# A decoder layer on one core: negated attention scores, and the second half's left output projection ahead of the first norms

## The chip, the cores and the metric

The kernel runs on one core of a Trainium2 chip. The metric is the device time of one execution in microseconds (us); lower is better. The kernel before takes 1022.47 us, the median of 3 runs (1022.22 to 1023.44). The engines are PE (TensorE), DVE (VectorE), ACT (ScalarE), POOL (GpSimd) and SP (SyncE, which here only issues DMAs). Each works off its own queue of instructions in order.

## The reference

One layer of a hybrid decoder on 1024 tokens of width 1024, in float32:

```python
z = h @ w_in                       # pool group | q | k | v
y_pool = pool_mixer(u_pool, w_pool, pool_scale)        # windows 2, 4, 8, 16
y_attn = sliding_window_attention(q, k, v, sinks)      # 128-token band
h = layer_norm(ALPHA * h + concat([y_pool, y_attn]) @ w_out)
h = layer_norm(ALPHA * h + square(relu(h @ w_ff1)) @ w_ff2)
h = h + sigmoid(h @ w_ple_gate + b_ple_gate) * (p @ w_ple)
```

In the attention each head has a sink, a score without a key:

```python
m = maximum(max(scores, axis=-1), sink)
e = exp(scores - m)
probs = e / (sum(e, axis=-1) + exp(sink - m))
```

## The kernel before

The tokens are handled in 8 blocks of 128 (n = 0 to 7), in two halves t of four. Every matrix product is made of three matmuls (`mm3`, lines 112 to 114): an operand is split into a rounded high part, cast on ACT (`high`, line 98), and a low part, the rest, subtracted on DVE or POOL (`low`, line 103). So a line of a trace with L98 or L103 is such a split, of whatever tile.

The stages around the change, in the order in which the program is written: query, key, value and pooling products; `attention(0)` to `attention(7)` with pooling groups between; `out_left(0)`, the left 512 columns of the output projection of blocks 0 to 3; `out_right(0)` to `(3)`, the right 512 columns; the first norms `norm1(0)` to `(3)`; `out_left(1)` and `out_right(4)` to `(7)` for the second half; then `early(0)` to `(7)`, the first products of the feed-forward part, with `norm1(4)` to `(7)` among them. A scheduler, which runs a timeline of its own, decides how instructions of neighbouring stages are mixed on each engine; it isn't a plain copy of the program's order.

`attention(n)` handles two groups of four heads. For each pair of heads there is one score tile s in PSUM (a single buffer): matmuls L283 and L284, then on DVE L287 adds the bias, takes the maximum with the sink and leaves it in `st`. L293 negates the four maxima, four exponentials (L295, ACT) use them as their bias, and DVE normalises (L299, L301); the transposes L308 follow on PE. The pooling groups use POOL and DVE for their window sums (L352, L355) and PE for `mm<-tmp,wp`.

`residual(n, ...)` (L427, DVE) adds the projection to ALPHA times the tokens in `hn[n]`, a tile of the pool "n" (`nat`, 8 buffers), one half of the columns at a time. `layer_norm` takes statistics (L393, L395) and the variance v (L397), its power -0.5 on POOL (L398), some small DVE instructions (L400 to L403), the centring on ACT (L404), and scale and shift on DVE (L405, L117). `norm1(n)` then transposes `hn[n]` in two groups of four on PE (L414), into a tile pt and a tile av in PSUM, and empties each of them by a plain copy to `raw[c]`, a high part and a low part into `X["11"]` and `X["21"]` (L513 to L516). `raw[c]` is itself a tile of the pool "n". At the end of `norm1` `hn[n]` is multiplied by ALPHA (L529, ACT) and stored to DRAM as `h_dram[n]` by a DMA that POOL issues (L530; in the profile hd). `early(0)` multiplies by the whole of `X["11"]`, so by all four blocks of the first half.

`out_left(1)` needs four weight tiles w (two buffers). In before each is loaded to a staging tile of the pool "ws", which exists only once the attention's buffers (`pa_ctx`) have been given back.

Of the kernel before, what the change touches and what calls it, by code (L numbers as in the profile page):

```python
# [7 lines left out]
F32 = mybir.dt.float32  # L8
F32R = mybir.dt.float32r
AF = mybir.ActivationFunctionType  # L10
ALU = mybir.AluOpType
# [56 lines left out]
def layer(ctx, tc, xT, x, pT, w_in, w_pool, pscale, sinks, w_out, ln1, w1, w2, ln2, w_ple, w_gate, bgate, bias, rcount, out):  # L68
# [14 lines left out]
    def wt(shape, dt=F32R):  # L83
        return sb.tile(shape, dt, tag="w", bufs=2, name=nm("w"))
# [179 lines left out]
    def attention(n):  # L264
# [4 lines left out]
        for g in range(2):  # L269
            e = pa.tile([P, 4, 2 * P + 1], F32, tag="e", bufs=2, name=nm("e"))  # L270
            st = small([P, 16])
            for j in range(2):
# [12 lines left out]
                for i in range(2):  # L285
                    h = 4 * g + 2 * j + i
                    nc.vector.tensor_tensor_reduce(  # L287
                        out=e[:, 2 * j + i, k0 : 2 * P], in0=s[:, i, k0 : 2 * P], in1=nd[:, k0 : 2 * P],
                        scale=SLOPES[h], scalar=sink_sb[:, h : h + 1], op0=ALU.add, op1=ALU.max,
                        accum_out=st[:, 2 * j + i : 2 * j + i + 1],  # L290
                    )
            nc.gpsimd.tensor_copy(out=e[:, :, 2 * P], in_=sink_sb[:, 4 * g : 4 * g + 4])
            nc.vector.tensor_scalar(out=st[:, 4:8], in0=st[:, 0:4], scalar1=-1.0, scalar2=None, op0=ALU.mult)  # L293
            for i in range(4):
                nc.scalar.activation(  # L295
                    out=e[:, i, k0 : 2 * P + 1], in_=e[:, i, k0 : 2 * P + 1], func=AF.Exp,
                    bias=st[:, 4 + i : 5 + i], scale=1.0, accum_out=st[:, 8 + i : 9 + i],
                )
# [82 lines left out]
    keys(0, first[0])  # L381
    nc.sync.dma_start(out=sink_sb, in_=sinks.partition_broadcast(P))
    nc.sync.dma_start(out=psc, in_=pscale)
    nc.sync.dma_start(out=rc, in_=rcount.partition_broadcast(P))
# [32 lines left out]
    def out_load(dst, dh, kk, st, eng):  # L417
        load_split(dst[:, 0], dst[:, 1], w_out[dh, kk], None, eng, st)
# [10 lines left out]

    def left_weights(kk, staging, eng):  # L430
        w = wt([P, 2, 2, HALF])
        out_load(w, 0, kk, staging(), eng)
        return w

    def out_left(t, staging, eng, ws=()):
        blocks = range(4 * t, 4 * t + 4)
        os = [acc_ps() for _ in blocks]
        for k in range(NK):
            if k % 2 == 0:
                w = ws[k // 2] if k // 2 < len(ws) else left_weights(k // 2, staging, eng)  # L440
            for n in blocks:
                out_mm(os[n % 4], n, k, w)
        return os

    def residual_left(t, os):
        for n in range(4 * t, 4 * t + 4):
            hn[n] = nat([P, D])
            nc.sync.dma_start(out=hn[n], in_=x[n * P : (n + 1) * P, :])
        for n in range(4 * t, 4 * t + 4):
            residual(n, 0, os[n % 4])  # L450
# [55 lines left out]
    def norm1(n):  # L506
        t, c = n // 4, n % 4
        layer_norm(hn[n], gb1)
        a = transposed(hn[n], 0, tr_ps())
        b = transposed(hn[n], 1, tr_av())  # L510
        if t == 0:
            raw[c] = nat([P, 2, 4, P])
# [4 lines left out]
        else:  # L517
# [10 lines left out]
            split_to("T4", c, t2, nc.gpsimd)  # L528
        nc.scalar.mul(out=hn[n], in_=hn[n], mul=ALPHA)  # L529
        nc.gpsimd.dma_start(out=h_dram[n], in_=hn[n])  # L530

# [16 lines left out]
    def early(p):  # L548
# [13 lines left out]
        return rest  # L562

    residual_left(0, out_left(0, lambda: stage([P, 2, HALF]), nc.gpsimd))
    for j in range(2):
# [9 lines left out]
    X["11"], X["21"] = (big([P, 2, 4, HALF]) for _ in range(2))  # L575
    by_part = (lambda: part((P, 2, HALF), F32), nc.vector)
    ws = [left_weights(kk, *by_part) for kk in range(2)]
    for n in range(4):
        norm1(n)
    residual_left(1, out_left(1, *by_part, ws))  # L580
    for n in range(4, NT):
# [343 lines left out]
```

## Time and profile before

| | |
|---|---|
| median of 3 runs | 1022.47 us |
| the profiled execution's own time | 1020.45 us |
| its span | 1018.7 us (1.75 us lie around it) |
| mean granted clock of TensorE | 0.992 |
| PE busy in the span | 994.7 us |

Times inside the execution are us from the span's start. A row of a timeline gives start, duration, engine, line, operation, output and inputs, the count of merged instructions, and in brackets the engine's idle time before it and what ended it. Rows of the waits give total, count and longest. A matmul of 512 columns shows 0.39 us, but the next one starts some 0.23 us later, since they overlap.

### The profile page before, as it was taken

What the parts mean: (1) busy time and instruction counts of PE and PEld (TensorE: products, weight loads), DVE (VectorE), ACT (ScalarE), POOL (GpSimd) and SP (SyncE); (2) the same over time, 40 slices, a digit from 0 to 9 for tenths busy, and PEclk for the clock granted to TensorE, in tenths of its full rate; (3) what the DMA queues carried; (4) which work ended last, traced back from release to release, by engine and by line L of the source; (5) the groups of instructions that cost most, each with busy time, mean ns of one, the idle gap of its engine ahead of it and who ended that gap; (6) DMA issues with size and microseconds to landing.
All of it is one profiled execution on the core that took longest, in us unless ns stands there. A gap on an engine that the chain in (4) does not pass through costs nothing.

```text
span 1018.7 us, 12237 instructions
## 1 busy us (share of the span) xinstructions
PE 994.7 (98%) x4556; PEld 824.0 (81%) x4556; DVE 707.4 (69%) x1115; ACT 458.3 (45%) x737; POOL 149.9 (15%) x180
## 2 busy tenths in 40 slices
PE   8999998989999999999999999999999999999998
PEld 6878886867888888888888888878788888888887
DVE  5778877793889676665456757787447799897433
ACT  5656656554277343443443444333433353651111
POOL 0043273620034000110000001000111120000000
PEclk9999999998999999999999999999999999999999
DMA  6421411416235233663264793656898773521011
GB/s 214 174 83 43 167 42 42 135 42 216 83 137 199 104 110 134 234 179 145 65 251 159 290 329 112 178 180 194 235 212 208 191 184 124 184 88 50 32 42 42
DMA packets 39004, 148.54 MB, mean 146 GB/s; under 512 B 4768, under 2 KB 5664, under 8 KB 36128
## 3 DMA queue, kind: packets, MB, share of 16 engines
q1 hardware_dynamic: 29664, 116.29, 33.3%
q0 software_dynamic: 9280, 31.46, 12.2%
q8 instruction: 36, 0.59, 0.2%
q14 instruction: 24, 0.20, 0.1%
HBM read 124.66 MB, written 23.07 MB: 145 GB/s over the span
## 4 chain that ended last, share of the span: by engine, by line
PE 84%; DVE 8%; DMA 5%; issue 2%; ACT 1%; POOL 0%; SPq 0%; DVEq 0%; ACTq 0%; POOLq 0%
PE f L113 20%; PE f L114 20%; PE f L112 20%; PE mm L112 7%; PE mm L113 7%; PE mm L114 6%; DMA ws<-in_w 3%; DMA w<-in_w 1%; DVE w L103 1%; DVE x L103 1%; PE pt L308 1%; DVE ws L117 1%; PE f L414 1%; PE s L283 1%; PE s L284 1%
## 5 line engine op out<-in xcount | busy, mean ns | idle before, releaser
L113 PE MATMUL f<-x,w 128*128 128x512 f32 x448 | 175.4, 392 | 3.6 <-DVE x L103 3.6
L113 PE MATMUL f<-c,ws 128*128 128x512 f32 (+1 forms) x456 | 175.9, 386 | 0.3 <-DVE c L103 0.3
L112 PE MATMUL f<-c,ws 128*128 128x512 f32 (+1 forms) x456 | 175.3, 385 | 0.0
L114 PE MATMUL f<-x,w 128*128 128x512 f32 x448 | 175.1, 391 | 0.0
L114 PE MATMUL f<-c,ws 128*128 128x512 f32 (+1 forms) x456 | 173.7, 385 | 0.0
L112 PE MATMUL f<-x,w 128*128 128x512 f32 x448 | 147.7, 390 | 0.0
L98 ACT CAST w<-st 128x1024 fp32r<-128x1024 f32 (+2 forms) x67 | 66.8, 998 | 114.3 <-issue 70.6
L103 DVE TENSOR_TENSOR w<-st,w 128x1024 fp32r<-128x1024 f32 (+2 forms) x63 | 74.9, 1192 | 43.0 <-ACT w L98 42.9
L113 PEld LDWEIGHTS f<-x,w 128*128 128x128 f32 x448 | 84.5, 189 | 22.0 <-DVE x L103 4.4
L113 PEld LDWEIGHTS f<-c,ws 128*128 128x128 f32 x456 | 85.7, 188 | 17.8 <-DVE c L103 0.7
L114 PEld LDWEIGHTS f<-c,ws 128*128 128x128 f32 x456 | 85.7, 188 | 17.2
L112 PEld LDWEIGHTS f<-c,ws 128*128 128x128 f32 x456 | 85.7, 188 | 17.1
L114 PEld LDWEIGHTS f<-x,w 128*128 128x128 f32 x448 | 84.5, 189 | 17.6
L112 PEld LDWEIGHTS f<-x,w 128*128 128x128 f32 x448 | 84.3, 188 | 17.4
L98 ACT CAST ws<-w 128x512 fp32r<-128x512 f32 x64 | 39.4, 621 | 59.5 <-PE f L114 45.9
L103 DVE TENSOR_TENSOR x<-ws,x 128x1024 fp32r<-128x1024 f32 x52 | 63.4, 1218 | 0.0
L112 PE MATMUL mm<-c,w 128*128 128x512 f32 x152 | 60.6, 403 | 1.0 <-ACT w L98 1.0
L113 PE MATMUL mm<-c,w 128*128 128x512 f32 x152 | 60.6, 400 | 0.4 <-DVE c L103 0.4
L114 PE MATMUL mm<-c,w 128*128 128x512 f32 x152 | 59.8, 398 | 0.0
L103 DVE TENSOR_TENSOR ws<-w,ws 128x512 fp32r<-128x512 f32 x64 | 46.0, 722 | 19.5 <-ACT ws L98 19.0
L98 ACT CAST ws<-st 128x512 fp32r<-128x512 f32 x48 | 29.8, 620 | 59.5 <-PE f L114 50.1
L117 DVE TENSOR_TENSOR n<-t,f 128x512 f32<-128x512 f32 x48 | 32.2, 683 | 32.0 <-PE f L114 32.0
(190 smaller groups left out, 1849.2 us busy)
## 6 DMA issues: line engine op xcount, KB each, us to landing
ws<-in_w SPq DMA_DIRECT2D x68, 512.0 KB, 3.5
w<-in_w SPq DMA_DIRECT2D x16, 1024.0 KB, 5.6
c<-fd SPq DMA_DIRECT2D x6, 2048.0 KB, 8.2
fd<-n POOLq DMA_DIRECT2D x20, 512.0 KB, 3.5
ws<-in_w POOLq DMA_DIRECT2D x20, 512.0 KB, 7.2
st<-in_w_in SPq DMA_DIRECT2D x18, 512.0 KB, 3.4
w<-in_w SPq DMA_DIRECT2D x12, 512.0 KB, 3.8
n<-in_x SPq DMA_DIRECT2D x8, 512.0 KB, 4.5
```

The lines of the kernel that those rows point to most:

```text
L98: nc.scalar.copy(out=dst, in_=src)
L103: eng.tensor_tensor(out=dst, in0=src, in1=hi.bitcast(F32), op=ALU.subtract)
L112: nc.tensor.matmul(o, ah, bh, start=first, stop=False, skip_group_check=more)
L113: nc.tensor.matmul(o, ah, bl, start=False, stop=False, skip_group_check=more)
L114: nc.tensor.matmul(o, al, bh, start=False, stop=last, skip_group_check=more)
L117: nc.vector.tensor_tensor(out=o, in0=a, in1=b, op=op)
L283: nc.tensor.matmul(s[:, i, dst], ql, kt[:, 0, g, kk : kk + kn], start=True, stop=False)
L284: nc.tensor.matmul(s[:, i, dst], ql, kt[:, 1, g, kk : kk + kn], start=False, stop=True)
L308: nc.tensor.transpose(pt[:, i, :], e[:, i, kb * P : (kb + 1) * P], ident)
L414: nc.tensor.transpose(pt[:, k, :], y[:, kt * P : (kt + 1) * P], ident)
```

## The change

Two things change. First, the scores are negated: the sinks are multiplied by -1 once after their load, L287 scales by -SLOPES and takes the minimum, and the exponential gets scale -1. The minimum is itself the bias that is wanted, so L293 goes; and each exponential can start on its own reduce.

Second, `out_left(1)` is written ahead of `norm1(0)`, and its weights are staged in tiles of the pool "n", whose buffers come free as query tiles die during the last attention block. The loads of the tokens (`residual_load`) become a step of their own behind it. In `norm1` the multiplication by ALPHA and the store to `h_dram` come right after the transposes, ahead of the copies to `raw[c]`.

```diff
@@ -286,15 +286,14 @@
                     h = 4 * g + 2 * j + i
                     nc.vector.tensor_tensor_reduce(
                         out=e[:, 2 * j + i, k0 : 2 * P], in0=s[:, i, k0 : 2 * P], in1=nd[:, k0 : 2 * P],
-                        scale=SLOPES[h], scalar=sink_sb[:, h : h + 1], op0=ALU.add, op1=ALU.max,
+                        scale=-SLOPES[h], scalar=sink_sb[:, h : h + 1], op0=ALU.add, op1=ALU.min,
                         accum_out=st[:, 2 * j + i : 2 * j + i + 1],
                     )
             nc.gpsimd.tensor_copy(out=e[:, :, 2 * P], in_=sink_sb[:, 4 * g : 4 * g + 4])
-            nc.vector.tensor_scalar(out=st[:, 4:8], in0=st[:, 0:4], scalar1=-1.0, scalar2=None, op0=ALU.mult)
             for i in range(4):
                 nc.scalar.activation(
                     out=e[:, i, k0 : 2 * P + 1], in_=e[:, i, k0 : 2 * P + 1], func=AF.Exp,
-                    bias=st[:, 4 + i : 5 + i], scale=1.0, accum_out=st[:, 8 + i : 9 + i],
+                    bias=st[:, i : i + 1], scale=-1.0, accum_out=st[:, 8 + i : 9 + i],
                 )
             nc.vector.reciprocal(out=st[:, 12:16], in_=st[:, 8:12])
             for i in range(4):
@@ -380,6 +379,7 @@
     first = z_first()
     keys(0, first[0])
     nc.sync.dma_start(out=sink_sb, in_=sinks.partition_broadcast(P))
+    nc.vector.tensor_scalar(out=sink_sb, in0=sink_sb, scalar1=-1.0, scalar2=None, op0=ALU.mult)
     nc.sync.dma_start(out=psc, in_=pscale)
     nc.sync.dma_start(out=rc, in_=rcount.partition_broadcast(P))
     nc.sync.dma_start(out=nd, in_=bias)
@@ -427,25 +427,23 @@
         nc.vector.scalar_tensor_tensor(out=v, in0=v, scalar=ALPHA, in1=o, op0=ALU.mult, op1=ALU.add)
 
 
-    def left_weights(kk, staging, eng):
-        w = wt([P, 2, 2, HALF])
-        out_load(w, 0, kk, staging(), eng)
-        return w
-
-    def out_left(t, staging, eng, ws=()):
+    def out_left(t, staging, eng):
         blocks = range(4 * t, 4 * t + 4)
         os = [acc_ps() for _ in blocks]
         for k in range(NK):
             if k % 2 == 0:
-                w = ws[k // 2] if k // 2 < len(ws) else left_weights(k // 2, staging, eng)
+                w = wt([P, 2, 2, HALF])
+                out_load(w, 0, k // 2, staging(), eng)
             for n in blocks:
                 out_mm(os[n % 4], n, k, w)
         return os
 
-    def residual_left(t, os):
+    def residual_load(t):
         for n in range(4 * t, 4 * t + 4):
             hn[n] = nat([P, D])
             nc.sync.dma_start(out=hn[n], in_=x[n * P : (n + 1) * P, :])
+
+    def residual_left(t, os):
         for n in range(4 * t, 4 * t + 4):
             residual(n, 0, os[n % 4])
 
@@ -508,6 +506,8 @@
         layer_norm(hn[n], gb1)
         a = transposed(hn[n], 0, tr_ps())
         b = transposed(hn[n], 1, tr_av())
+        nc.scalar.mul(out=hn[n], in_=hn[n], mul=ALPHA)
+        nc.gpsimd.dma_start(out=h_dram[n], in_=hn[n])
         if t == 0:
             raw[c] = nat([P, 2, 4, P])
             nc.scalar.copy(out=raw[c][:, 0], in_=a)
@@ -526,8 +526,6 @@
             split_to("T3", c, r12, nc.vector)
             nc.gpsimd.tensor_tensor(out=t2, in0=raw[c][:, 1], in1=t2, op=ALU.subtract)
             split_to("T4", c, t2, nc.gpsimd)
-        nc.scalar.mul(out=hn[n], in_=hn[n], mul=ALPHA)
-        nc.gpsimd.dma_start(out=h_dram[n], in_=hn[n])
 
     def w_split(src):
         s = part()
@@ -561,6 +559,7 @@
 
         return rest
 
+    residual_load(0)
     residual_left(0, out_left(0, lambda: stage([P, 2, HALF]), nc.gpsimd))
     for j in range(2):
         w = big([P, 2, 2, 2, HALF])
@@ -573,11 +572,11 @@
     for n in range(4):
         out_right(n)
     X["11"], X["21"] = (big([P, 2, 4, HALF]) for _ in range(2))
-    by_part = (lambda: part((P, 2, HALF), F32), nc.vector)
-    ws = [left_weights(kk, *by_part) for kk in range(2)]
+    os = out_left(1, lambda: nat([P, 2, HALF]), nc.vector)
+    residual_load(1)
     for n in range(4):
         norm1(n)
-    residual_left(1, out_left(1, *by_part, ws))
+    residual_left(1, os)
     for n in range(4, NT):
         out_right(n)
     pre = wide("pre", [P, NPRE, HALF], F32)
```

What the engines' queues look like at three places. After the change line numbers up to L380 are one lower from L293 on, L414 and L427 keep theirs, and the norm's product and store are L509 and L510. Tiles: n_319 to n_322 are hn[0] to hn[3] in before, n_307 to n_310 after; n_369 to n_372 and n_349 to n_352 are hn[4] to hn[7].

PE in before, at the end of attention(7); w_337 is the first weight tile of out_left(1), pt and av are the norms' transposes:

```order
L313 MATMUL av_301_1825<-pp_305_1841,k_26_227 128x512
L414 MATMUL pt_343_2139<-ident_61,n_319_1975 128x128 x4
L314 MATMUL av_301_1825<-pp_305_1841,k_26_227 128x512
L414 MATMUL pt_348_2172<-ident_61,n_320_1977 128x128 x4
L414 MATMUL av_344_2144<-ident_61,n_319_1975 128x128 x4
L414 MATMUL pt_353_2205<-ident_61,n_321_1979 128x128 x4
L414 MATMUL av_349_2177<-ident_61,n_320_1977 128x128 x4
L414 MATMUL pt_358_2238<-ident_61,n_322_1981 128x128 x4
L414 MATMUL av_354_2210<-ident_61,n_321_1979 128x128 x4
L112 MATMUL mm_361_2257<-w_337_2115,c_243_1527 128x512
L112 MATMUL mm_362_2258<-w_337_2115,c_243_1527 128x512
L112 MATMUL mm_363_2259<-w_337_2115,c_243_1527 128x512
```

PE after, at the same place; w_341 is that first weight tile, av_301 the last of the attention:

```order
L113 MATMUL mm_334_2072<-c_326_1981,c_66_477 128x512
L114 MATMUL mm_334_2072<-c_326_1981,c_66_477 128x512
L112 MATMUL mm_337_2100<-w_341_2104,c_243_1516 128x512
L313 MATMUL av_301_1810<-pp_303_1816,k_26_228 128x512
L312 MATMUL av_301_1810<-pp_305_1826,k_26_228 128x512
L113 MATMUL mm_337_2100<-w_341_2104,c_243_1516 128x512
L114 MATMUL mm_337_2100<-w_341_2104,c_243_1516 128x512
L112 MATMUL mm_338_2101<-w_341_2104,c_243_1516 128x512
L313 MATMUL av_301_1810<-pp_305_1826,k_26_228 128x512
L113 MATMUL mm_338_2101<-w_341_2104,c_243_1516 128x512
L114 MATMUL mm_338_2101<-w_341_2104,c_243_1516 128x512
L112 MATMUL mm_339_2102<-w_341_2104,c_243_1516 128x512
```

The transposes of the norms have gone from here, and out_left(1) follows the attention directly. They stand among and behind out_left(1) and out_right(4) to (7) now. The end of out_right(7) after the change, PE (mm_376 is out_right(7), mm_386 early(0), pt_389 and pt_406 belong to hn[4] and hn[5]):

```order
L113 MATMUL mm_376_2442<-c_326_1981,c_205_1314 128x512
L114 MATMUL mm_376_2442<-c_326_1981,c_205_1314 128x512
L414 MATMUL pt_370_2341<-ident_61,n_310_1846 128x128 x4
L414 MATMUL av_366_2313<-ident_61,n_309_1844 128x128 x4
L414 MATMUL pt_389_2510<-ident_61,n_349_2220 128x128 x4
L414 MATMUL av_371_2346<-ident_61,n_310_1846 128x128 x4
L414 MATMUL pt_406_2630<-ident_61,n_350_2222 128x128 x4
L112 MATMUL mm_386_2482<-c_335_2098,ws_384_2476 128x512
L112 MATMUL mm_397_2548<-c_335_2098,ws_395_2542 128x512
```

In before out_right(7) is followed by early(0) without any transposes of the first half. Now those of hn[3] and half of those of hn[2] stand between them. At that time POOL's queue in before holds the four stores of the first half and then the four powers of the second:

```order
L530 DMA hd0_75<-n_319_1975 128x1024
L530 DMA hd1_76<-n_320_1977 128x1024
L530 DMA hd2_77<-n_321_1979 128x1024
L530 DMA hd3_78<-n_322_1981 128x1024
L398 TENSOR_TENSOR sm_388_2514<-sm_388_2514,mhalf_66 128x1
L398 TENSOR_TENSOR sm_405_2634<-sm_405_2634,mhalf_66 128x1
L398 TENSOR_TENSOR sm_422_2754<-sm_422_2754,mhalf_66 128x1
L398 TENSOR_TENSOR sm_439_2874<-sm_439_2874,mhalf_66 128x1
L530 DMA hd4_79<-n_369_2367 128x1024
```

POOL after:

```order
L510 DMA hd0_75<-n_307_1840 128x1024
L398 TENSOR_TENSOR sm_388_2499<-sm_388_2499,mhalf_66 128x1
L510 DMA hd1_76<-n_308_1842 128x1024
L398 TENSOR_TENSOR sm_405_2619<-sm_405_2619,mhalf_66 128x1
L398 TENSOR_TENSOR sm_422_2739<-sm_422_2739,mhalf_66 128x1
L398 TENSOR_TENSOR sm_439_2859<-sm_439_2859,mhalf_66 128x1
L510 DMA hd2_77<-n_309_1844 128x1024
L510 DMA hd3_78<-n_310_1846 128x1024
L510 DMA hd4_79<-n_349_2220 128x1024
```

The stores of hn[2] and hn[3] have moved behind the last power. And ACT after, from the centring of hn[6] on (n_367 and n_372 are raw[2] and raw[3], c_335 is X["11"], c_336 is X["21"]):

```order
L404 ACTIVATE n_351_2224<-n_351_2224,sm_422_2739 128x1024
L509 ACTIVATE n_309_1844<-n_309_1844 128x1024
L404 ACTIVATE n_352_2226<-n_352_2226,sm_439_2859 128x1024
L513 COPY n_367_2320<-pt_365_2308 128x512
L98 CAST c_335_2098<-pt_365_2308 128x4x128
L515 COPY n_367_2320<-av_366_2313 128x512
L98 CAST c_336_2099<-av_366_2313 128x4x128
L519 COPY t_391_2522<-pt_389_2510 128x512
L509 ACTIVATE n_310_1846<-n_310_1846 128x1024
L98 CAST c_379_2470<-t_392_2523 128x4x128
L513 COPY n_372_2353<-pt_370_2341 128x512
L98 CAST c_335_2098<-pt_370_2341 128x4x128
```

In before the copies of hn[2] and hn[3] stand ahead of all centrings of the second half. Now the copies to raw[2] and raw[3] (L513) stand behind them, and each waits for the landing of the store of the block whose slot it takes.

The third place is the scores ahead of out_left(0). PE in before (mm_285 is a pooling group, mm_307 the first of out_left(0), s_248 a score tile of attention(6)):

```order
L308 MATMUL pt_222_1414<-ident_61,e_215_1376 128x128
L308 MATMUL pt_220_1404<-ident_61,e_215_1376 128x128
L308 MATMUL pt_222_1414<-ident_61,e_215_1376 128x128
L283 MATMUL s_248_1540<-k_154_983,n_137_861 128x256
L284 MATMUL s_248_1540<-k_154_983,n_137_861 128x256
L283 MATMUL s_248_1540<-k_154_983,n_137_861 128x256
L284 MATMUL s_248_1540<-k_154_983,n_137_861 128x256
L112 MATMUL mm_285_1740<-tmp_284_1737,wp_95 128x512
L112 MATMUL mm_307_1855<-w_311_1859,c_150_950 128x512
L113 MATMUL mm_307_1855<-w_311_1859,c_150_950 128x512
```

PE after (mm_311 is the first of out_left(0)):

```order
L307 MATMUL pt_220_1394<-ident_61,e_215_1367 128x128
L307 MATMUL pt_222_1404<-ident_61,e_215_1367 128x128
L113 MATMUL mm_285_1727<-tmp_284_1724,wp_95 128x512
L114 MATMUL mm_285_1727<-tmp_284_1724,wp_95 128x512
L283 MATMUL s_247_1522<-k_154_976,n_133_819 128x256
L284 MATMUL s_247_1522<-k_154_976,n_133_819 128x256
L283 MATMUL s_247_1522<-k_154_976,n_133_819 128x256
L284 MATMUL s_247_1522<-k_154_976,n_133_819 128x256
L112 MATMUL mm_311_1848<-w_315_1852,c_150_943 128x512
L113 MATMUL mm_311_1848<-w_315_1852,c_150_943 128x512
```

s_248 has moved behind the first 25 matmuls of out_left(0), and s_247 now comes after the transposes.

## The prediction

> **What bounds the kernel now.** I read the busy shares of the page first.
>
> ```profile
> PE 994.7 (98%) x4556; PEld 824.0 (81%) x4556; DVE 707.4 (69%) x1115; ACT 458.3 (45%) x737; POOL 149.9 (15%) x180
> ```
>
> TensorE is the bound, and the change takes no matmul away. It can win only where PE idles and lose only where it makes PE idle anew. So the next view is who PE waits for, over the stretch that the change reorders (140 to 300 us), and then the same for 60 to 80 us.
>
> ```profile
> PE s L283 <- DVE sm L287: 3.4, 2, 2.2
> PE av L414 <- DVE y L317: 2.9, 1, 2.9
> PE pt L414 <- DVE n L117: 2.6, 2, 2.0
> ...
> PE s L283 <- DVE sm L287: 1.3, 2, 1.0
> PE pt L308 <- DVE e L301: 0.5, 1, 0.5
> ```
>
> The reader is to see two sorts: score matmuls (L283) that wait for the reduces of the score tile before, and the transposes of the first norms (L414). The second sort, in the timeline of PE with the windows of PE around it (time, PE busy, instructions, granted clock, DMA share, GB/s):
>
> ```profile
> 231.58 1.12 PE L414 MATMUL pt<-ident,n 128*128 128x128 f32 x4 [2.01 <-DVE n L117]
> 232.49 1.06 PE L414 MATMUL av<-ident,n 128*128 128x128 f32 x4
> ...
> 276.26 0.39 PE L113 MATMUL mm<-c,c 128*128 128x512 f32 x1
> ...
> 278.07 0.39 PE L112 MATMUL mm<-c,ws 128*128 128x512 f32 x1
> ...
> 222.10:278.07 55.97, 49.83 (x224) 0.94 0.43 151
> 228.00:234.85 6.85, 4.39 (x16) 0.50 0.85 336
> ```
>
> From the end of attention (222.10) to the first matmul of early(0) (278.07) PE issues 224 instructions in 55.97 us: 32 transposes and 192 matmuls of out_left(1) and out_right(4) to (7). A 512-column matmul is issued every 0.227 us (the rows of 276.26 and 278.07 are eight issues apart, 1.81); a group of four transposes took 0.91 from start to start at half clock (231.58 to 232.49), so 0.44 or 0.11 each at full clock. So 192 x 0.227 + 32 x 0.11 = 43.6 + 3.5 = 47.1 us of work, and **8.9 us are lost**, in gaps and in the half clock that follows them.
>
> **The change part by part.**
>
> (1) The norms leave this place. Out_left(1) now follows attention on PE, its weights staged in the slots of dead query tiles. Their first load waits for score matmuls of attention(7) that stand some 130 matmuls, over 25 us, ahead of out_left(1); a load of that size takes 3.4, its cast 1.05 (row further down), its low part 1.22 (as L117 of the same width).
>
> ```profile
> st<-in_w_in SPq DMA_DIRECT2D x18, 512.0 KB, 3.4
> ```
>
>  That is 5.7 in 25, so I cost it at nothing; DVE takes the two low parts earlier, ahead of score reduces that PE needs some 2 us later. Without that cover it would be up to 2.4 us. If all else followed without a wait, early(0) would start 8.9 earlier.
>
> (2) It does not follow. raw[c] now takes the slot of hn[c], so its first copy (L513) waits until hn[c] has landed in h_dram, and the PSUM tile that it empties is wanted by the next transposes. T is the end of out_right(7): 222.1 + 43.6 + 5 groups of transposes x 0.44 = 267.9. Up to there the copies of hn0 and hn1 lie beside matmuls (slack about 1 us at hn1). But in POOL's queue the store of hn2 stands behind the four powers L398 of hn4 to hn7, and the last needs out_right(7). The rows for this chain, of DVE, POOL and ACT, from the same work in before:
>
> ```profile
> 278.27 0.69 DVE L427 SCALAR_TENSOR_TENSOR n<-n,mm 128x512 f32<-128x512 f32 x1 [0.56 <-PE mm L114]
> ...
> 279.72 0.21 DVE L395 BATCH_NORM_AGGREGATE sm<-sm 128x2 f32<-128x12 f32 x1
> 279.85 1.28 DVE L405 SCALAR_TENSOR_TENSOR n<-n,sm,st 128x1024 f32<-128x1024 f32 x1
> ...
> 281.18 1.22 DVE L117 TENSOR_TENSOR n<-n,st 128x1024 f32<-128x1024 f32 x1
> ...
> 276.91 0.55 POOL L398 TENSOR_TENSOR sm<-sm,mhalf 128x1 f32<-128x1 f32 x1 [5.36 <-DVE sm L403]
> 281.28 1.52 POOL L398 TENSOR_TENSOR sm<-sm,mhalf 128x1 f32<-128x1 f32 x1 [3.82 <-DVE sm L403]
> 284.88 0.58 POOL L530 DMA_DIRECT2D hd<-n  x1 [2.08 <-ACT n L529]
> ...
> 283.53 1.05 ACT L529 ACTIVATE n<-n 128x1024 f32<-128x1024 f32 x1
> ...
> L98 ACT CAST w<-ws 128x1024 fp32r<-128x1024 f32 x4 | 4.1, 1053 | 5.8 <-PE mm L114 5.8
> L98 ACT CAST c<-pt 128x512 fp32r<-128x512 f32 x4 | 2.4, 603 | 0.0
> ...
> L513 ACT COPY n<-pt x4: 585/591/602, 222.4 to 233.4; 128x512 f32<-128x512 f32 x4
> ...
> L103 DVE TENSOR_TENSOR c<-pt,c 128x512 fp32r<-128x512 f32 x4 | 2.7, 682 | 0.0
> ```
>
> The landing times of the store (tile hd), for 222 to 236, 236 to 250 and 290 to 325 us:
>
> ```profile
> DMA to landing us min/median/max: 3.5/4.3/5.2
> DMA to landing us min/median/max: 2.9/3.8/4.7
> DMA to landing us min/median/max: 2.9/2.9/3.4
> ```
>
> Step by step from T. Residual, statistics, aggregate and v: T+0.2 to T+2.0 (278.07 to 279.93 above, with v next). Power: 0.55 alone, 1.52 beside a 1024-wide DVE instruction; now L405 of hn6 stands right behind v on DVE, so I take 1.52: T+3.5. The store of hn2 is issued there and lands in 2.9, as in the quiet stretch, since no load is under way then: T+6.4. ACT copies and casts both halves of hn2, four times about 0.52 back to back: T+8.5, and the DVE low part 0.68: T+9.1. The transposes of hn3 need that PSUM tile: 0.44, T+9.6. The product with ALPHA 1.08: T+10.7; 0.30 to the store (283.53 + 1.05 to 284.88), and 2.9: T+13.9. First copy, cast and low part of hn3: 0.5 + 0.6 + 0.68: T+15.7. Only then is X["11"] whole, and early(0) is the next on PE. That is 267.9 + 15.7 = 283.6 against 278.07: +5.5. Two groups of transposes (hn4, hn5) that PE did later in before are paid in it: -0.9. And PE, idle for some 13 us in pieces, comes back at the half clock: +1.7, as below. **Norm part +6.3, I take +6.5.** Ends: power 0.55, +5.3; both landings at 5.2 (the crowded stretch), +10.9. DVE's own queue (L405 and L117 of hn6 and hn7, 5.0 us from T+2.0) ends at about T+7.2, ahead of the low part at T+8, so it is not late.
>
> (3) The scores. Sixteen negations L293 go and one of 128x8 comes, on sinks loaded at the start.
>
> ```profile
> L293 DVE TENSOR_SCALAR sm<-sm x16: 152/240/1235, 46.4 to 206.8; 128x4 f32<-128x4 f32 x16
> ...
> DMA to landing us min/median/max: 6.0/6.0/6.0
> ```
>
> A median of 0.24 each, off PE's path in most places: nothing from that alone. The one new instruction lies between 0.15 and 1.24 by these rows, and I take 0.24, off the path. It waits for the sinks' load, which lands 6.0 after its issue (last row); ahead of all low parts that could cost 6.0, but it stands behind ten of them, so I take no wait. What counts is that the scheduler places the attention section anew. In before:
>
> ```profile
> 153.38 0.28 PE L283 MATMUL s<-k,n 128*128 128x256 f32 x1
> ...
> 155.02 0.50 PE L313 MATMUL av<-pp,k 128*128 128x512 f32 x1 [1.00 <-DVE y L317]
> ...
> 159.38 0.39 PE L283 MATMUL s<-k,n 128*128 128x256 f32 x1 [2.22 <-DVE sm L287]
> ...
> 164.10 0.39 PE L283 MATMUL s<-k,n 128*128 128x256 f32 x1 [1.22 <-DVE sm L287]
> ...
> 165.12 0.39 PE L112 MATMUL mm<-w,c 128*128 128x512 f32 x1
> ...
> 153.62 0.69 DVE L355 SCALAR_TENSOR_TENSOR h<-h,h 128x512 f32<-128x512 f32 x1
> ...
> 156.29 2.23 DVE L355 SCALAR_TENSOR_TENSOR h<-h,h 128x512 f32<-128x512 f32 x1
> 158.44 0.47 DVE L287 CUSTOM_DVE_ANT_0 e<-s,nd,sink_sb 128x256 f32<-128x256 f32 x1
> ...
> 159.76:163.17 3.41, 3.12 (x14) 0.50 0.27 106
> ```
>
> 4.4 us of gaps, and 3.41 us at half clock, worth 1.7. After the change s_248, whose wait is the last of them, stands behind 25 matmuls of out_left(0). Five more rows stand ahead of s_227 (153.38 becomes 154.5); L354 then holds DVE for its slow 2.23 (to 156.7), two reduces of 0.47 follow (157.7), then s_228, the normalisation with its transposes (159.7, the reduces of s_228 behind it), and s_247 at 160.6: out_left(0) starts at about 161.1 instead of 165.12, with the same work done but for s_248 (0.48 owed) and two matmuls of mm_285 (0.45 paid). That is -4.0; -5.5 if L354 takes its usual 0.69; -2.3 if the half clock falls behind those gaps too. I take **-3.0**. At 69 to 72 us the reorder touches waits of 1.8 in all: 0, between -1.8 and +1.8.
>
> Half a clock is a rule too: the Trainium skill ("TensorE: Matmul & The Clock Gate", What's actually happening) says that an idle window of about 3.4 us halves the clock until a busy one has passed. This trace agrees: 3.41 us at 0.50. It speaks against the change, since one long gap pays it as surely as several short ones; by it the term is 3.41 x 0.5 = 1.7, the same as by the row, and without it the norm part would be +4.8.
>
> **The sum.** +6.5 - 3.0 + 0 = +3.5. The profiled execution took 1020.45 (span 1018.7), so 1023.95; the median of the runs shown is 2.0 higher, 1022.47, and on that footing **1026.0**.
>
> **The rivals.**
> - *Hidden after all*: out_left(1) and out_right(4) to (7) cover the norms, early(0) starts at T + 1.3. For it: in 236 to 268 us DVE and ACT are busy less than half the time (14.45 and 9.14 of 32 us in the window below). It decides itself at POOL's order: hn2's store would have to be issued before the last power. The price is -8.9 - 3.0 = -11.9: 1010.6, faster. The order stands against it. 0.12.
>
> ```profile
> 236.00:268.00 32.00, 32.00 (x145) 26.50 (x144) 14.45 (x26) 9.14 (x13) 1.62 (x3) 1.00 0.50 176
> ```
>
> - *Even*: the attention part brings its best (-5.5) and the chain its cheapest (+5.3): 1022.3. Needs L354 and the power both undisturbed. 0.16.
> - *Slow landings*: stores of hn2 and hn3 land in 5.2 as at 229 to 232 us, each paid in full, and hn1's slack goes: +10.9 - 3.0 + 1 = +8.9, 1031.4. In before the DMA share there was 0.85 (the window above), and now no load is under way. The Trainium skill ("SBUF — State Buffer", SBUF: two separate sides) has a rule for it: DVE can lock POOL out of a shared port so that POOL cannot write a transfer's descriptors. The trace half agrees: a power took 1.52 instead of 0.55 beside L117, but the store at 284.88 beside L405 cost 0.58. 0.12.
> - *It does not do what it says*: staging lands late and out_left(1) waits at 222 as the norms did, and the chain comes on top: up to +8.9 more, 1035. 0.03.
> - My forecast, +0.2 to +7: 0.57.
>
> **How the numbers follow.** About 2 us (0.2%) can be told from no change by measurements of this kernel. Faster by more: the hidden case and a tail of the even one, 0.17. Within: most of the even one and the forecast's low end, 0.20. Slower: 0.63. The range leaves out the hidden case and the far end of the slow ones: 1019 to 1031.
>
> **What would show it.** PE without a gap at 222 to 234, and mm<-w,c right behind the attention's last matmuls; then, at about 268, gaps of some 12 us in pieces ahead of the first mm<-c,ws, put down to casts and copies that wait for the DMA of hd, with two landings near 2.9 one after the other; the clock at 0.50 behind them; out_left(0) at about 161. Wrong if L513 of hn3 waits for nothing, if the store of hn2 comes before the last power, or if the gaps before 165 remain.

## The result and the profile after

The changed kernel takes 1032.02 us, the median of 6 runs (1028.57 to 1033.99), against 1022.91 (1022.22 to 1023.5) for the kernel before beside it. The ratio is 1.0088, with a 95% interval of 1.0071 to 1.0106: **slower by about 9 us**. The forecast was slower by 3.5, and 1032.02 lies 1 us outside the range. The profiled execution took 1033.38 us with a span of 1031.6.

First the busy row of the page of the changed kernel, and below it the waits of PE over the whole span (total, count, longest).

```profile
PE 999.5 (97%) x4556; PEld 826.1 (80%) x4556; DVE 705.5 (68%) x1100; ACT 460.0 (45%) x737; POOL 152.5 (15%) x180
```

```profile
PE pt L414 <- DVE c L103: 7.8, 1, 7.8
PE mm L112 <- ACT c L98: 4.0, 2, 3.7
PE s L283 <- DVE sm L287: 3.9, 2, 3.0
...
PE av L312 <- DVE y L316: 1.4, 1, 1.4
PE mm L112 <- ACT tmp L98: 1.2, 1, 1.2
PE pt L307 <- DVE e L300: 1.2, 3, 0.5
```

PE has as many instructions as before, but 4.8 us more of busy time (work at half clock) and new waits. Of the waits for the norms that before had, none is left. Two long ones took their place (the first two rows), and the waits of the attention have grown rather than shrunk (the last four rows: 7.7 us; in the same view of before L283 4.7, L313 1.0 and L308 0.5, 6.2 in all).

**Where the time went.** For each PE instruction of a trace I take its start and subtract the work ahead of it at the quiet spacing: 0.227 us for each matmul of 512 columns, 0.119 for 256, 0.112 for a transpose. What is left is the time PE has lost so far, in gaps and at half clock. This ledger is worked out from all 4556 rows of PE in each profiled execution:

| PE's loss in us | before | after | difference |
|---|---|---|---|
| up to the end of the attention (222 us) | 18.3 | 22.6 | +4.3 |
| at the norms, 222 to 234 us | 9.0 | 0.0 | -9.0 |
| from the norms up to early(0) and behind it | 0.0 | 16.1 | +16.1 |
| all later | 6.5 | 8.0 | +1.5 |

The sum, +12.9, is the difference of the two profiled executions (1033.38 - 1020.45). So there are two errors to explain: the norm part came out at +7.1 (forecast +6.5), and the attention part at +4.3 in this profile (forecast -3.0).

The windows of the changed kernel at the place of the old wait and at the new one (length, then busy time and instructions of PE, PEld, DVE, ACT and POOL, granted clock, DMA share, GB/s):

```profile
222.00:236.00 14.00, 14.00 (x64) 11.59 (x63) 12.35 (x23) 4.46 (x5) 3.59 (x3) 1.00 0.00 1
268.00:289.00 21.00, 8.84 (x41) 6.84 (x40) 14.99 (x29) 10.85 (x18) 3.16 (x4) 0.68 0.12 50
```

Out_left(1) fills 222 to 236 us without a gap. At 268 to 289 PE is busy for 8.84 of 21 us, and part of that at half clock. The timelines of PE, of ACT and of POOL there:

```profile
272.10 0.60 PE L414 MATMUL pt<-ident,n 128*128 128x128 f32 x4
...
280.96 1.11 PE L414 MATMUL pt<-ident,n 128*128 128x128 f32 x4 [7.83 <-DVE c L103]
281.87 1.06 PE L414 MATMUL av<-ident,n 128*128 128x128 f32 x4
...
288.38 1.65 PE L112 MATMUL mm<-c,ws 128*128 128x512 f32 x3 [3.73 <-ACT c L98]
```

```profile
278.94 0.59 ACT L513 COPY n<-pt 128x512 f32<-128x512 f32 x1 [2.09 <-DMA hd<-n]
...
282.97 1.06 ACT L509 ACTIVATE n<-n 128x1024 f32<-128x1024 f32 x1 [0.21 <-PE av L414]
...
287.25 0.59 ACT L513 COPY n<-pt 128x512 f32<-128x512 f32 x1 [2.72 <-DMA hd<-n]
```

```profile
274.45 1.55 POOL L398 TENSOR_TENSOR sm<-sm,mhalf 128x1 f32<-128x1 f32 x1 [1.37 <-DVE sm L397]
275.96 0.57 POOL L510 DMA_DIRECT2D hd<-n  x1
284.32 0.53 POOL L510 DMA_DIRECT2D hd<-n  x1 [7.79 <-ACT n L509]
```

The chain is to be read across the three: the last power (274.45), the store of hn2 (275.96), its landing 2.9 us later, the copy to raw[2] (278.94), the second transposes of hn3 (281.87; the first ran at 272.10, and the group at 280.96 is hn4's), the product with ALPHA (282.97), the store of hn3 (284.32), its landing, the copy to raw[3] (287.25), and early(0) at 288.38. With T = 272.1 that is T + 16.3.

### The profile page after: what moved, and what is told of

The parts are those of the page before. It is cut to its first block, busy times and chain, and to the rows that moved or that the text cites. A ratio compares the mean times of both kernels' runs of the same rounds, so it can differ in the third digit from the quotient of the medians.

```text
span 1031.6 us, 12204 instructions
## 1 busy us (share of the span) xinstructions
PE 999.5 (97%) x4556; PEld 826.1 (80%) x4556; DVE 705.5 (68%) x1100; ACT 460.0 (45%) x737; POOL 152.5 (15%) x180
## 3 DMA queue, kind: packets, MB, share of 16 engines
q0 software_dynamic: 9280, 31.46, 12.3%
## 4 chain that ended last, share of the span: by engine, by line
PE 71%; issue 14%; DVE 7%; DMA 5%; POOL 2%; ACT 2%; SPq 0%; POOLq 0%; DVEq 0%; ACTq 0%
PE f L113 16%; PE f L114 16%; PE f L112 15%; PE mm L112 6%; PE mm L113 6%; PE mm L114 6%; DMA ws<-in_w 3%; DVE e L300 1%; PE pt L307 1%; DVE w L103 1%; DVE x L103 1%; DMA hd<-t 1%; PE f L414 1%; PE s L284 1%; PE s L283 1%
## 5 line engine op out<-in xcount | busy, mean ns | idle before, releaser
L114 PEld LDWEIGHTS f<-c,ws 128*128 128x128 f32 x456 | 85.7, 188 | 17.1
L112 PEld LDWEIGHTS f<-c,ws 128*128 128x128 f32 x456 | 85.7, 188 | 17.1
```

The costliest lines, as they stand in the source:

```text
L112: nc.tensor.matmul(o, ah, bh, start=first, stop=False, skip_group_check=more)
L114: nc.tensor.matmul(o, al, bh, start=False, stop=last, skip_group_check=more)
```

## The experiments

Theories. **Two landings**: the norm part alone makes the kernel slower, since X["11"] waits for two stores to land one after the other. **The order**: negating the scores makes the scheduler place the attention anew, and this new order costs time. Rivals: the arithmetic (minimum, scale -1) costs; the stores are late because of POOL's queue, not of the landing; nothing in the attention costs at all.

The last two columns are the ledger of each profiled execution: what PE lost up to the end of the attention (222 us), and from there to the same point of PE's work (330 us in before). Each ratio is to executions of before that were taken beside the run; their medians were 1021.61 to 1022.91 (the first row is one of them), so runs are compared by the ratios. A ledger is of one execution only.

| run | median us | ratio to before | lost to 222 | lost 222 to 330 |
|---|---|---|---|---|
| before | 1022.91 | | 18.3 | 9.8 |
| the change | 1032.02 | 1.0088 (1.0071 to 1.0106) | 22.6 | 17.1 |
| e1 negated only | 1022.15 | 1.0012 (0.9993 to 1.0031) | 20.5 | 8.2 |
| e2 staged only | 1028.99 | 1.0078 (1.0053 to 1.0103) | 21.0 | 17.6 |
| e3 negated, old order | 1021.82 | 1.0007 (0.9995 to 1.0019) | 19.3 | 9.8 |
| e4 store without hn | 1020.06 | 0.9987 (0.9971 to 1.0002) | 21.6 | 5.4 |
| e5 norms between | 1023.85 | 1.0024 (1.0014 to 1.0035) | 20.3 | 12.7 |
| e6 e5, negated | 1027.68 | 1.0055 (1.0040 to 1.0070) | 22.4 | 12.3 |
| e7 store by ACT | 1032.36 | 1.0101 (1.0082 to 1.0121) | 22.1 | 16.5 |
| e8 loads among norms | 1019.41 | 0.9978 (0.9962 to 0.9994) | 21.3 | 7.8 |
| e9 second norms earlier | 1015.12 | 0.9939 (0.9926 to 0.9952) | 18.4 | 3.5 |
| e10 e8, negated | 1017.67 | 0.9958 (0.9942 to 0.9974) | 23.1 | 2.9 |
| e11 e9, negated | 1016.76 | 0.9953 (0.9935 to 0.9970) | 21.9 | 1.4 |
| e12 e11, old order | 1015.79 | 0.9950 (0.9933 to 0.9966) | 17.8 | 3.4 |

**The two halves apart: e1 and e2.** e1 is the kernel before with the five lines on the scores changed as in the diff, and nothing else; e2 has the rest of the diff and the old scores.

> The kernel before with the negated scores alone. On PE and DVE the attention section then stands in the order of the changed kernel up to about 196 us, and out_left(1) stays behind the norms. Theory 'order' (the scheduler's new order of the attention section, not the staged weights, cost 4.3 us in the trace of the changed kernel): 1025.5 to 1028, out_left(0) starting at about 167.5. Rival 'staging' (casts and low parts of the staged weights cost it): 1022.9, out_left(0) at 165.1.

> The kernel before with the second part alone: staged weights and out_left(1) ahead of the first norms, scores as before. PE's order up to the end of attention is that of before. Theory 'two landings' (the norms' chain behind out_right(7) costs 7.2 net): 1029 to 1031, attention ends at 222, early(0) starts at about 285 with two waits of L513 for the store. Rival 'staging': attention ends 4 us later here too, 1032 to 1034.

e2: 1.0078, so +8.0 us, with the same two waits (its PE waits from 222 us on):

```profile
PE pt L414 <- DVE c L103: 7.6, 1, 7.6
PE mm L112 <- ACT c L98: 3.7, 1, 3.7
```

The staging alone carries nearly the whole loss, and two landings stands. e1 missed what the order theory expected: no time lost that can be measured (1.0012, 0.9993 to 1.0031), and out_left(0) at 165.26, not 167.5. But its ledger shows why that settles less than it seems: PE lost 2.2 us more ahead of the norms and 2.0 less at them (7.0 instead of 9.0). The waits of PE at 222 to 235 us, first of before, then of e1:

```profile
PE av L414 <- DVE y L317: 2.9, 1, 2.9
PE pt L414 <- DVE n L117: 2.6, 2, 2.0
PE av L414 <- DVE c L103: 0.6, 1, 0.6
```

```profile
PE pt L414 <- DVE sm L403: 4.7, 1, 4.7
```

The sum goes from 6.1 to 4.7. The end of that wait is set by a chain on DVE, ACT and POOL; a PE that arrives later waits less. So the wait of before can take up a delay (or a saving) that arises ahead of it, and the changed kernel has no such wait there.

**Order or arithmetic: e3.** A copy on DVE takes the place of the instruction that goes, so every engine keeps the order of before (but for the product of the sinks with -1 at the start, on DVE):

```diff
-            nc.vector.tensor_scalar(out=st[:, 4:8], in0=st[:, 0:4], scalar1=-1.0, ...)
+            nc.vector.tensor_scalar(out=st[:, 4:8], in0=st[:, 0:4], scalar1=1.0, ...)
```

> The scores negated, but one DVE instruction still copies the four minima and the exponentials take the copies as bias: PE, ACT and POOL then have exactly the order of before. Theory 'order': 1022 to 1023.5, no difference. Rival 'arithmetic' (the minimum, the negative scale or the single negation of the sinks cost time themselves): 1025 or more.

1.0007, within 0.2% of before: minimum, sign and scale cost nothing that can be measured.

**What the landing costs: e4 and e7.** In e4 the first four stores take a tile that nobody overwrites; what is stored to `h_dram` for the first half is then not the norm's result, and that part of the output is not computed:

```diff
-        nc.gpsimd.dma_start(out=h_dram[n], in_=hn[n])
+        nc.gpsimd.dma_start(out=h_dram[n], in_=hn[n] if t else gb1[0])
```

> The changed kernel, but the stores of the first four blocks take the norm's scale instead of hn, so no copy to raw waits for a landing (the stored values are left out, the rest of the work is there). Theory 'two landings': early(0) starts about 4 us after the end of out_right(7) instead of 16.3, so 1018 to 1021. Rival 'norms of the second half' (DVE's queue of normalisations and the powers hold the copies, whatever the stores do): 1029 or more, L513 of hn3 still 12 us or more after out_right(7).

1020.06, inside the expected range, and 1.0% (10 us) under the changed kernel in the ratios. PE's waits in e4 from 222 to 300 us:

```profile
PE pt L414 <- DVE t L117: 1.3, 1, 1.3
PE mm L113 <- DVE c L103: 0.7, 1, 0.7
PE mm L112 <- ACT c L98: 0.4, 1, 0.4
```

Ahead of and behind early(0) PE loses 5.0 instead of 16.1. But more than the waits for the landings has changed. The four stores now need nothing of the norms, and the scheduler has them issued 50 to 80 us earlier (count, durations in ns, first and last start):

```profile
L510 POOL DMA_DIRECT2D hd<-st x4: 533/595/784, 200.5 to 202.5; - x4
```

It also mixes the norms anew: the second transposes of hn2 run at 267.36, among out_right(7), and its product with ALPHA at 267.99, ahead of the centring of hn6 (271.43), while in the changed kernel it comes behind that (273.54). So e4 shows what it costs that the copies depend on the stores at all: 11.1 us in the ledger. The two landings of 2.9 make up 5.8 us of the chain; how the rest divides between the late place of the stores and the order that follows from it was not tried apart.

In e7 the changed kernel's first four stores are issued by ACT, so that no power on POOL stands ahead of them:

```diff
-        nc.gpsimd.dma_start(out=h_dram[n], in_=hn[n])
+        (nc.scalar if t == 0 else nc.gpsimd).dma_start(out=h_dram[n], in_=hn[n])
```

> The changed kernel, the stores of the first four blocks issued by ACT right behind their product, so not behind the powers in POOL's queue. Theory 'two landings': the store of hn2 comes 1.3 us earlier and little else changes: 1030 to 1032 (the changed kernel: 1032.0). Rival 'POOL's queue': the place behind the last power is what costs: 1028 or less.

No gain (1.0101), with 6.5 and 4.2 us for the two waits of the first fence. The store of hn2 is issued 2.5 us behind the end of out_right(7) (274.08) instead of 3.9 (275.96), and nothing that can be measured comes of it. So POOL's queue is not the cause; that the copies wait for stores is. In ACT's queue the store of hn2 still stands behind the centring of hn6 (271.95); a store ahead of that was not tried.

**A version without the two landings: e5 and e6.** Old scores. The four staging loads of out_left(1) are issued ahead of it, and norm1(0) to (3) run one by one between its four pairs of k, so that the copies to raw take the slots that the staging tiles leave, not those of hn:

```diff
+            if between and k % 2:
+                between(k // 2)
...
-    os = out_left(1, lambda: nat([P, 2, HALF]), nc.vector)
+    os = out_left(1, lambda: nat([P, 2, HALF]), nc.vector, norm1)
     residual_load(1)
-    for n in range(4):
-        norm1(n)
```

> Scores as before; the weights of out_left(1) staged in the pool n, all four loads ahead, and norm1(0) to (3) written between its pairs of k. raw then takes the slots of the staging tiles, and no copy waits for a store. Theory 'hidden': nothing waits at 222 nor ahead of early(0); the 8.9 us of before go: 1012 to 1015. Rival 'norms too late': DVE has not finished hn1 to hn3 when PE reaches their transposes, gaps of 2 to 5 us inside out_left(1): 1016 to 1020.

> As the run before, with the negated scores. Theory 'absorbed': the negated order costs PE some 2 us in the attention section, which the wait for the norms hid in the kernel with negated scores alone; without that wait it shows: 1.5 to 3 us above the run before. Rival 'free': within 1 us of the run before.

e5 met neither expectation: both old stalls are gone, and a new one stands between. The PE waits of e5 from 222 to 300 us, and its SP timeline:

```profile
PE mm L112 <- DVE n L427: 5.9, 1, 5.9
PE av L414 <- DVE c L103: 2.5, 1, 2.5
```

```profile
242.43 7.23 SPq L559 DMA_DIRECT2D w<-in_w  x3
249.71 0.90 SPq L455 DMA_DIRECT2D n<-in_x  x2
```

The residual of hn4 (L427) waits for its tokens. Their load is issued at 249.71 only, behind three loads of feed-forward weights that themselves wait for slots: the queue of SP works in order. e6 came out 3.8 us above e5 in the medians (0.31% in the ratios), more than the 1.5 to 3 of its expectation. Not all of that is the attention: between the two profiled executions the ledger has +2.2 up to 222 us, -0.4 from there to 330, and +2.7 behind it, where e5 lost less than any other kernel.

**The load in its place: e8, then e9.** e8 issues the loads of hn[4] to hn[7] inside the interleaving, ahead of the weights':

```diff
+    def between(n):
+        if n < 3:
+            norm1(n)
+        hn[4 + n] = nat([P, D])
+        nc.sync.dma_start(out=hn[4 + n], in_=x[(4 + n) * P : (5 + n) * P, :])
+        if n == 3:
+            norm1(n)
```

> Old scores; norm1(n) between the pairs of out_left(1) as in the run before the last, but the loads of hn[4] to hn[7] are issued among them, ahead of the loads of w1. Theory (the only thing wrong there was the place of hn[4]'s load in SP's queue): the wait of L427 at 249 to 258 goes, PE has no gap over 2 us between 220 and 290, early(0) stands directly behind out_right(7), and of the 8.98 us that before loses at 222 to 231 at least 6 are saved: 1012 to 1016 us. Rival (the residuals of hn[4] to hn[7] wait for hn[0] to hn[3]'s stores to land, since they take their slots, or the norms' chain ends too late ahead of early(0)): a new wait of 3 to 8 us behind out_right(4) or ahead of early(0), and 1018 to 1023 us.

The waits between 220 and 315 us are gone, as the theory had it, but the time is 1019.41, not 1012 to 1016: 7 us came back from 317 us on, where the feed-forward part starts: two waits of 3.3 in all, and the half clock from 323.0 to 329.8 for most of the rest. PE's timeline there:

```profile
322.81 0.65 PE L112 MATMUL f<-c,ws 128*128 128x512 f32 x1 [2.12 <-ACT c L98]
324.67 0.80 PE L113 MATMUL f<-c,ws 128*128 128x512 f32 x1 [1.22 <-DVE c L103]
```

The splits of hn[7] come last on DVE and ACT. e9 spreads the norms of the second half over early(1) to (4):

```diff
-        if p % 2 and p // 2 < 4:
-            norm1(4 + p // 2)
+        if p <= 4:
+            norm1(3 + p)
```

> The last kernel with norm1(4) to norm1(7) at early(1) to (4) instead of (1), (3), (5), (7). The last kernel's profile has no gap at 220 to 315 us but 4.95 us at 317 to 325, where the first products of the feed-forward part wait for DVE's splits of hn[7] and of the first weights. Theory (the splits of the second half's norms come last on DVE there): with them earlier, at least 3 of those 4.95 go, no new wait over 2 us between 270 and 325: 1014.5 to 1016.5 us. Rival (the landing of the weights sets it: the loads wait for slots): the gaps stay within 1.5 us, 1018 to 1020.5; or early(1) and early(2) now wait for hn[4] and hn[5], up to 1025.

1015.12 us, ratio 0.9939: faster than both kernels, by about 6 and 15 us in the ratios. It is inside the expected range; only the wait of 2.1 us below (at 310.87) is longer than the 2 that were allowed for. The page's busy row and the waits of PE from 200 to 330 us:

```profile
PE 992.7 (98%) x4556; PEld 822.0 (81%) x4556; DVE 710.6 (70%) x1115; ACT 458.3 (45%) x737; POOL 151.8 (15%) x180
```

```profile
PE mm L112 <- ACT t L553: 2.1, 1, 2.1
PE mm L112 <- ACT pre L563: 0.3, 1, 0.3
```

**The negated scores where less can take up their delay: e10 to e12.** e10 is e8 with the five lines of e1, e11 is e9 with them, e12 is e9 with those of e3 (negated, old order).

> The kernel of the run before (loads of hn[4] to hn[7] among the norms) with negated scores, so without the norms' wait at 222 us that could take up a delay. If the new order of the attention costs by itself: 2 to 4.5 us above that kernel's 1019.4, so 1021.4 to 1024, with out_left(0) later than in it and PE's extra losses ahead of 222 us. If it costs nothing (as it seemed with the old norms, 1022.15 against 1021.61): within 1 us of 1019.4. If it saves the 3.0 of the prediction: 1016.4.

> The fastest kernel so far (1015.12, second norms earlier; no wait at 222 us and none ahead of the feed-forward part but 2.5 us) with negated scores: little is left behind the attention that could take up a delay. If the new order of the attention costs by itself what its traces show ahead of 222 us (4.1 to 4.7 us there in four of the profiles): 1018 to 1020. If the absorbed cost was not real: 1014.5 to 1015.8. If the prediction's saving of 3.0 at out_left(0) exists: 1012.

> The same with negated arithmetic in the old order: a copy on DVE keeps the place of the instruction that went, so only scale, minimum and sign differ from the fastest kernel. If the cost is the order's: 1014.5 to 1016, and 2.5 to 5 us under the run before. If it is the arithmetic's (minimum, scale -1): as the run before.

e10 missed all three cases: 0.2% under e8. Its ledger loses 1.8 us more up to 222, but 4.9 less behind it, so that the wait at 317 us of e8 took the delay up, and more. e11 (1016.76) lies between its cases too, 1.0 us above e12, with overlapping intervals, where 2.5 to 5 had been expected; in the profiles it lost 4.1 more up to 222 and 2.0 less behind it. e12 lies 0.11% above e9 and e11 0.14%, so in the time these runs show no cost of the order beside the arithmetic.

So the same five lines were put on five kernels (the ratios with them less those without): e1 on before +0.12%, the change on e2 +0.10%, e6 on e5 +0.31%, e10 on e8 -0.20%, e11 on e9 +0.14%. The mean is +0.09%, 1.0 us; with a spread this wide it is not clear of zero, and none shows the -3.0 of the prediction. Only e6 on e5 is clearly above zero, and in the profiles more than half of that lies behind 330 us. That the new order costs PE time within the attention is shown by the ledgers: 20.5 to 23.1 us in the seven profiles with it (mean 22.0), 17.8 to 21.3 in the seven with the old order (19.5). The clock fits this: around 160 to 169 us it was at half for 6.8 us in all seven with the new order, and for 3.4 us in five and 6.8 in two of those with the old one; at 73 to 77 us it was at half for another 3.4 us in six of the seven with the new order and in none with the old. How much of these 2.5 us reaches the end depends on the wait behind them; a number that holds for any kernel is not shown.

## Why the prediction was wrong

**The direction and the mechanism of the norm part were right.** Out_left(1) took the place of the norms, and the 8.9 us went. The chain ran as it was written down: power 1.52 forecast, 1.55 measured; landings 2.9 and 2.9; two of them one after the other. T + 15.7 forecast, T + 16.3 measured. The difference comes from the product with ALPHA (282.97, T + 10.9 instead of T + 9.6): it waited for the transposes, for which I had counted one group of 0.44, and two groups ran at the half clock (one of hn4 at 280.96, then hn3's at 281.87). The end won 0.7 back, since early(0) started behind the first cast, 1.1 us after the landing, and not behind the low part, 1.8. In the ledger the part is +7.1, in the time of e2 +8.0 (5.4 to 10.5): right in its mechanism, a little small. The rival of slow landings gave 1031.4, near the result, but its mechanism did not occur.

**The step that failed is "I take -3.0" for the scores.** It rested on out_left(0) starting at 161.1 instead of 165.12. It started at 167.46, and the gaps ahead of 165 remained, which the prediction had named as a sign of being wrong. In the ledger the stretch from 150 to 170 us, where the 3.0 were to be saved, loses as much as in before: 7.3 instead of 7.1. PE, DVE and POOL of the changed kernel there:

```profile
158.24 0.28 PE L283 MATMUL s<-k,n 128*128 128x256 f32 x1
...
161.87 0.39 PE L283 MATMUL s<-k,n 128*128 128x256 f32 x1 [3.00 <-DVE sm L287]
...
163.38 1.09 PE L307 MATMUL pt<-ident,e 128*128 128x128 f32 x4 [0.54 <-DVE e L300]
164.84 1.11 PE L307 MATMUL pt<-ident,e 128*128 128x128 f32 x4 [0.37 <-DVE e L300]
...
166.60 0.41 PE L283 MATMUL s<-k,n 128*128 128x256 f32 x1
...
167.46 0.63 PE L112 MATMUL mm<-w,c 128*128 128x512 f32 x1
```

```profile
158.18 2.83 DVE L354 SCALAR_TENSOR_TENSOR h<-h,h 128x512 f32<-128x512 f32 x1 [0.45 <-POOL h L351]
...
162.66 2.39 DVE L300 TENSOR_SCALAR e<-e,sm 128x256 f32<-128x256 f32 x4
```

```profile
158.11 2.36 POOL L103 TENSOR_TENSOR w<-st,w 128x1024 fp32r<-128x1024 f32 x1
161.79 1.29 POOL L103 TENSOR_TENSOR tmp<-h,tmp 128x512 fp32r<-128x512 f32 x1 [1.33 <-ACT tmp L98]
163.36 1.28 POOL L103 TENSOR_TENSOR c<-y,c 128x512 fp32r<-128x512 f32 x1 [0.28 <-ACT c L98]
```

The order is the one that the prediction read, and its first wait is there. But two things were wrong in it:

- *The start.* s_227 was put at 154.5 and stands at 158.24. The 3.7 us are delays from further ahead, which I had set at 0, between -1.8 and +1.8 (69 to 72 us), or had not looked at (98 us). PE's timeline of the changed kernel shows them:

```profile
70.33 0.38 PE L283 MATMUL s<-k,n 128*128 128x256 f32 x1 [0.91 <-DVE sm L287]
...
72.49 0.47 PE L312 MATMUL av<-pp,k 128*128 128x512 f32 x1 [1.42 <-DVE y L316]
...
99.45 0.50 PE L112 MATMUL mm<-tmp,wp 128*128 128x512 f32 x1 [1.23 <-ACT tmp L98]
```

  In the ledger that is +2.6 at 69 to 73 us (waits and the half clock behind them) and +1.2 at 98 us. The wait at 98 us is in the profile of every kernel with the new order, and in none with the old one.
- *The durations.* From s_227 to out_left(0) I had 6.6 us; it took 9.2. L354 took 2.83 instead of 2.23, the four normalisations 2.39 instead of the 1.14 that they took in before, where POOL was idle beside them. The rest is the clock: PE ran at half speed from 162.8 to 169.6, behind the first gap, for 6.8 us where before had 3.4. The prediction had named a half clock here as the bad end of this term (-2.3), not as its likeliest value, and had it last 3.4:

```profile
162.80:169.60 6.80, 5.89 (x21) 4.80 (x21) 6.27 (x16) 5.95 (x15) 1.75 (x3) 0.50 0.02 9
```

  The half clock needed no idle window of 3.4 us, which the rule cited in the prediction asks for: PE's longest gap in the 3.4 us ahead of a half clock was 2.22 us in before (159.8), and 1.42 in the changed kernel (74.0).

So a stretch of 7 us was worked out with durations from the order before, though the new order puts other work beside it on POOL. No run moved POOL's instructions alone: that changes the order of the whole attention once more. But e8, which has before's order here, shows such a meeting. There the split on POOL started while the normalisations still ran, and they took 2.15 instead of 1.14. The reduces behind them came 1.0 later for it, and PE, whose transposes had also ended sooner, waited for them 2.99 instead of 1.22. DVE, POOL and PE of e8:

```profile
162.60 2.15 DVE L301 TENSOR_SCALAR e<-e,sm 128x256 f32<-128x256 f32 x4
162.96 1.38 POOL L103 TENSOR_TENSOR c<-y,c 128x512 fp32r<-128x512 f32 x1
165.61 0.38 PE L283 MATMUL s<-k,n 128*128 128x256 f32 x1 [2.99 <-DVE sm L287]
```

**The sum.** +7.1 and +4.3 and +1.5 of later waits give the +12.9 of the two profiles. In the medians the norm part is about +8 and the scores about +1: against +6.5 and -3.0, four of the 5.5 us of error are the scores' and 1.5 the norms' (both measured to some 2 to 3 us only). The range was too narrow because each case above the forecast still had the scores at -3.0. The bounds that stood in the text, taken together, were 10.9 - 2.3 + 1.8 = +10.4, or 1032.9.

## What to carry to other kernels

A wait whose end another engine sets takes up delays that arise ahead of it (in e1's profile 2.2 us, of which 2.0 were taken up at the norms): whoever fills such a wait with work must look for what it had hidden. Where a new tile takes the slot of one that is being stored, the store's landing becomes a wait of the new tile's writer: give it a slot that a finished step leaves. And a load that the program moves must be followed through its DMA queue, since it stands behind every load that waits there for a slot.

## What was not expected of the hardware

**A DVE instruction can wait for one of POOL that has started.** L354 ended at 158.18 + 2.83 = 161.01, the split on POOL at 158.11 + 2.36 = 160.47: 0.54 later. In before, L355 ended at 156.29 + 2.23 = 158.52; the split beside it on POOL:

```profile
155.59 2.38 POOL L103 TENSOR_TENSOR w<-st,w 128x1024 fp32r<-128x1024 f32 x1
```

It ended at 157.97: 0.55 earlier. So the 2.23 that the prediction took for a slow duration was what was left of POOL's instruction plus 0.55 (alone it takes 0.69), and the price in the new order follows from POOL's start, not from the old row. Likewise the four normalisations, of 0.35 us each when alone: the third ran from 163.41 to 164.78, with POOL's split of c from 163.36 to 164.64, 0.14 earlier. An instruction that reads PSUM was not held: the split `pp<-pt,pp` at 154.89 in before took 0.67 beside POOL's L352 (154.57 to 155.63). The Trainium skill ("SBUF — State Buffer", SBUF: two separate sides) states that DVE and POOL share a pair of ports under an exclusive lock, held for a whole instruction, and that the loser blocks; these three rows agree with it. The prediction had used that rule for the stores only.

**The same order can lose 3 us more or less.** e3 has PE's order of before throughout; e2, e5, e8, e9 and e12 have it up to the end of the attention. They lost 19.3, 21.0, 20.3, 21.3, 18.4 and 17.8 us there, before 18.3. The window of 160 to 168 us of before and of e3 (granted clock third from the end):

```profile
160.00:168.00 8.00, 6.78 (x30) 5.28 (x30) 7.62 (x24) 5.68 (x15) 2.80 (x3) 0.80 0.08 34
```

```profile
160.00:168.00 8.00, 6.43 (x23) 5.24 (x23) 7.31 (x23) 5.49 (x14) 2.81 (x3) 0.57 0.02 7
```

PE's gaps are alike, but the clock was at half from 159.8 to 163.2 in before and from 160.3 to 167.1 in e3: 30 instructions of PE were done in one window, 23 in the other. In e2 and e8 it was at half for 3.4 us only, but later (from 165.7 and 166.0). At full clock the transposes ahead of that ended sooner (eight in 1.20 us in e8, 1.91 in before), so POOL's split behind them started sooner too and met DVE's normalisations, as in the rows of e8 above. One profile is therefore a weak measure of a term of 2 us, which is why the ledger's means and the ratios stand above.
